# Four heads' 16x16 triangles inverted in one batch, a block per partition, in a two-layer DeltaNet and attention trunk on one core

## The chip, the cores and the metric

The kernel runs on one core of one Trainium2 chip. The number that counts is the device time of one execution in microseconds. A core has TensorE (PE in the profile, with its weight loads as PEld), VectorE (DVE), ScalarE (ACT), GpSimd (POOL) and SyncE (SP); all of them run their own instruction lists in order and wait for each other by semaphores. DMAs are issued from an engine's list, before the change from SP's alone.

## The reference, cut to what matters

Two layers, 256 tokens, width 2048. In each layer the normed and modulated input is projected into the queries, keys, values and gates of eight DeltaNet heads and into sixteen attention heads; both kinds of output are concatenated, projected back and added; then comes a SwiGLU block. The part that the change touches is the inverse of a unit lower triangular matrix for each chunk of each head:

```python
lower = jnp.where(strict, jnp.einsum('bhncd,bhnsd->bhncs', kb, kc) * decay, 0.0) + eye
t_inv = lax.linalg.triangular_solve(lower, jnp.broadcast_to(eye, lower.shape),
                                    left_side=True, lower=True, unit_diagonal=True)
w = jnp.einsum('bhncs,bhnsd->bhncd', t_inv, kb * jnp.exp(gc)[..., None])
u = jnp.einsum('bhncs,bhnsd->bhncd', t_inv, vb)
```

The kernel cuts the 256 tokens into two chunks of 128 and so has two 128x128 triangles per head, each with eight 16x16 triangles on its diagonal.

## The kernel before, in words

All activations lie transposed, 128 features by 256 tokens. A weight block of 128x128 is split into a rounded part `wh` (a CAST on ACT) and the rest `wl` (a subtraction on DVE, sometimes on POOL), 512 columns at a time, and PE multiplies both parts with the split activations: two or three matmuls for a block (`mm2`, L663, and `mm3`, L656). DVE also makes the dot products of the modulation (`wada`, L576), the conv steps, the residual sums and most of the small steps of the heads.

The order of all engines' instructions is fixed when the program is built. `Timed` (L96) keeps a clock for each engine from prices of its own, and `Steps` (L217) holds the heads' steps as generators: at each tick between two weight blocks it lets those run whose engine has room by these clocks, and what they issue then stands at that place in the engine's list. Where the builder has nothing to issue for the next projection, because a buffer or a flag is missing, it calls `S.wait()` (L266), and only steps of the heads are put in until the flag is there. `Weights.split` (L336) puts the casts and subtractions up to five parts of four blocks ahead of PE.

The first layer's early projections are summed in stages while the modulation arrives (L1478). From about 250 us the heads of layer 0 run, then the output projection (`gemm_two`, L1532), then from 653 us the feed-forward block; layer 1 starts at 1377 us, its output projection at about 1768 us, its feed-forward block at 1850 us.

The projections go in the order of `JOBS` (L36 to L38): `ak` and `av` for attention's keys and values, two `aq`, and then for each DeltaNet head `k`, `q`, one `aq`, `v` and `z`. Within a layer the value projection of head h waits until head h-2 has set its flag `mid` (L1525), since the value tile has two buffers.

`delta` (L1163) is one DeltaNet head from its decay factors to its gated output:

- scores: two matmuls `g1`, `g2` with the keys as weights (L1196), then on DVE the norms (`junk`, `sk`), their reciprocal `sc` and the scaled and decayed matrices `B` (L1210). Two heads may be past this point at a time (`head`, `B` with two buffers).
- the triangles: DVE masks the diagonal blocks (`do`, L1228) and sums them into `mc`, 16 columns for each of 128 rows and two chunks (L1232); two more instructions make `R` (L1240), and a matmul with the constant `same` spreads each block's rows over its 16 partitions (L1246).
- the inverse: for each of the 15 columns and two chunks one multiply-and-sum on DVE into `uc` (L1254), and a read of its accumulator; 30 pairs that each need the one two before.
- merging: `U` spreads `uc` into block form (L1264), PE transposes U and the values v (L1275, L1277), and three rounds join blocks of 16 into 32, 64 and 128, with hops from PE to DVE or ACT and back at each (`y16`, `yn`, W).
- the rest: state, output, norm and gate; the matmuls with `V` (L1383) are the first that need the values.

SBUF tiles come from one pool; PSUM has one pool for each stage, `HEADS` and `FFN` (L168).

## Time and profile before

| | |
|---|---|
| median of 3 runs | 2602.87 us (2583.37 to 2609.12) |
| the profiled execution | 2606.06 us |
| its span, first to last instruction | 2604.2 us |
| around the span | 1.9 us |
| mean granted TensorE clock | 0.983 |

A row of a group gives the engine, the operation, output and inputs by the program's names, the shape, the count, the busy time and the mean of one. Since every operation is recorded through one helper, L155 stands at nearly all rows, and tiles tell them apart. A row of a table of stretches gives for each engine its busy time and the number of instructions, then the granted clock and the DMA engines' share. PE's records end by a model, and matmuls overlap in them, so PE's pitch is read from starts.

### The profile page before, as it was taken

What the parts mean: (1) busy time and instruction counts of PE and PEld (TensorE: products, weight loads), DVE (VectorE), ACT (ScalarE), POOL (GpSimd) and SP (SyncE); (2) the same over time, 40 slices, a digit from 0 to 9 for tenths busy, and PEclk for the clock granted to TensorE, in tenths of its full rate; (3) what the DMA queues carried; (4) which work ended last, traced back from release to release, by engine and by line L of the source; (5) the groups of instructions that cost most, each with busy time, mean ns of one, the idle gap of its engine ahead of it and who ended that gap; (6) DMA issues with size and microseconds to landing.
All of it is one profiled execution on the core that took longest, in us unless ns stands there. A gap on an engine that the chain in (4) does not pass through costs nothing.

```text
span 2604.2 us, 45895 instructions
## 1 busy us (share of the span) xinstructions
PE 2500.6 (96%) x16398; PEld 2148.0 (82%) x16398; DVE 1944.2 (75%) x4831; ACT 1281.5 (49%) x2759; POOL 417.9 (16%) x375
## 2 busy tenths in 40 slices
PE   6999999888999999999999899999899999999998
PEld 4777777777888888888888788998788888888887
DVE  3647777998777888888997877787877766555565
ACT  3225555335455444454445565644555544555553
POOL 2223333552000000000003443345000000000000
PEclk9999999999999999999999899999899999999999
DMA  8888664675777899999996433346577766555564
GB/s 279 294 286 290 241 211 171 222 253 187 259 253 252 311 323 323 324 328 330 324 346 204 163 123 121 130 162 203 194 265 249 261 187 188 196 190 188 184 195 137
DMA packets 184088, 608.62 MB, mean 234 GB/s; under 512 B 19121, under 2 KB 30513, under 8 KB 183857
## 3 DMA queue, kind: packets, MB, share of 16 engines
q1 hardware_dynamic: 183858, 605.68, 68.4%
q8 instruction: 128, 2.10, 0.3%
q14 instruction: 102, 0.84, 0.1%
HBM read 603.51 MB, written 2.10 MB: 233 GB/s over the span
## 4 chain that ended last, share of the span: by engine, by line
PE 42%; issue 30%; DVE 6%; ACT 1%; POOL 0%; POOLq 0%; DVEq 0%; ACTq 0%
PE pr L155 19%; PE psm L155 12%; PE pm L155 10%; DVE wl L155 1%; DVE wada L155 1%; DVE x L155 1%; ACT wh L155 0%; DVE act L155 0%; DVE R L155 0%; DVE mc L155 0%; DVE ry L155 0%; DVE sp_y L155 0%; DVE cv L155 0%; DVE do L155 0%; DVE B L155 0%
## 5 line engine op out<-in xcount | busy, mean ns | idle before, releaser
L155 ACT CAST wh<-w 128x512 fp32r<-128x512 f32 (+1 forms) x1566 | 900.9, 605 | 408.1 <-PE psm L155 137.7
L155 DVE TENSOR_TENSOR wl<-w,wh 128x512 fp32r<-128x512 f32 (+1 forms) x1317 | 893.3, 698 | 249.9 <-ACT wh L155 240.0
L155 PE MATMUL pr<-act,wh 128*128 128x512 f32 x2816 | 993.0, 397 | 10.8 <-DVE kq L155 7.5
L155 PE MATMUL pr<-act,wl 128*128 128x256 f32 x2816 | 792.8, 282 | 0.0
L155 PE MATMUL pm<-act,wh 128*128 128x256 f32 (+1 forms) x2816 | 658.6, 320 | 13.8 <-DVE x L155 5.0
L155 PEld LDWEIGHTS pr<-act,wh 128*128 128x128 f32 x2816 | 531.4, 189 | 137.5 <-DVE kq L155 8.1
L155 PE MATMUL psm<-act,wh 128*128 128x512 f32 (+1 forms) x1792 | 569.4, 373 | 1.8 <-ACT wh L155 0.9
L155 POOL TENSOR_TENSOR wl<-w,wh 128x512 fp32r<-128x512 f32 (+1 forms) x249 | 344.3, 1388 | 1272.0 <-ACT wh L155 1174.2
L155 PEld LDWEIGHTS pm<-act,wh 128*128 128x128 f32 x2816 | 462.7, 194 | 88.9 <-issue 44.6
L155 PEld LDWEIGHTS pr<-act,wl 128*128 128x128 f32 x2816 | 535.7, 190 | 0.0
L155 PE MATMUL pm<-act,wl 128*128 128x256 f32 x1664 | 474.3, 285 | 1.3 <-POOL wl L155 1.3
L155 PE MATMUL psm<-act,wl 128*128 128x256 f32 x1600 | 450.5, 282 | 1.7 <-POOL wl L155 1.7
L155 PEld LDWEIGHTS psm<-act,wh 128*128 128x128 f32 x1792 | 325.6, 190 | 72.5 <-issue 9.0
L155 DVE CUSTOM_DVE_ANT_0 wada<-wada,cs 128x1024 f32<-128x1024 f32 x256 | 325.5, 1274 | 36.6 <-DMA wada<-w_ada 36.2
L155 PEld LDWEIGHTS pm<-act,wl 128*128 128x128 f32 x1664 | 322.4, 194 | 2.2 <-POOL wl L155 1.7
L155 PEld LDWEIGHTS psm<-act,wl 128*128 128x128 f32 x1600 | 304.0, 190 | 2.7 <-POOL wl L155 2.1
L155 ACT COPY kq<-pr 128x512 f32<-128x512 f32 x88 | 51.8, 589 | 206.7 <-PE pr L155 206.6
L155 POOL TENSOR_TENSOR n2r<-ms,halfc 128x2 f32<-128x2 f32 x5 | 3.5, 691 | 797.9 <-DVE ms L155 797.9
L155 DVE TENSOR_TENSOR kq<-pr,kq 128x512 f32<-128x512 f32 x88 | 60.6, 688 | 92.8 <-ACT kq L155 92.8
L155 DVE SCALAR_TENSOR_TENSOR x<-psm,mod,x 128x256 f32<-128x256 f32 x128 | 61.9, 483 | 70.4 <-PE psm L155 67.9
L155 PE MATMUL psm<-wada,cs 128*32 128x256 f32 x1024 | 86.7, 414 | 17.7 <-DMA wada<-w_ada 17.5
L155 ACT CAST act<-kq 128x256 fp32r<-128x256 f32 x88 | 35.8, 407 | 74.0 <-DVE kq L155 74.0
(176 smaller groups left out, 1752.1 us busy)
## 6 DMA issues: line engine op xcount, KB each, us to landing
wada<-w_ada SPq DMA_DIRECT2D x384, 512.0 KB, 5.5
w<-w_gu SPq DMA_DIRECT2D x352, 512.0 KB, 4.6
w<-w_in SPq DMA_DIRECT2D x147, 512.0 KB, 4.0
w<-w_dn SPq DMA_DIRECT2D x128, 512.0 KB, 4.6
w<-w_out SPq DMA_DIRECT2D x64, 512.0 KB, 4.3
w<-w_dn SPq DMA_DIRECT2D x64, 384.0 KB, 4.2
w<-w_in SPq DMA_DIRECT2D x28, 384.0 KB, 4.9
x<-xT SPq DMA_DIRECT2D x4, 512.0 KB, 7.5
```

The costliest lines, as they stand in the source:

```text
L155: return f(*a, **k)
```

## The change

`delta` is cut in three. `scores` runs from the decay factors to `mc`, and now also squares the queries and sums them (`sq`, `qn`), so that a head's key and query tile is free after it. `inverses` takes the `mc` of four heads: eight DMAs from ACT's list bring each block of 16x16 into one partition of `qi` (64 partitions, one for each of 4 heads, 2 chunks and 8 blocks); DVE inverts all 64 at once, joining 2x2 into 4x4, 8x8 and 16x16 by products and sums; eight more DMAs from ACT's list bring the result back as `uc`, in the form that it had before. The DMA instructions stand in ACT's list between its casts. The new `delta` starts at `U`, and transposes the values only after the merging, where it also sets `mid`.

`JOBS` puts the keys and queries of four heads first; those of head h+4 come after `v` and `z` of head h. `B` has six buffers in place of two, `y16` two. To have room for it SBUF gets a pool for each stage, like PSUM: the heads' tiles and eight of the feed-forward's `act` tiles (now `mid`) lie in the same place at different times. The constants `same` and `nid16` are gone, and `own` carries the sign. The builder charges 2500 ns for each batch of DMAs (`nc.end += 2500`).

```diff
-NACT = 38
+NACT, NMID = 30, 8
 NEG = -1e30
 
 
-AHEAD = 2
+
+AHEAD, BATCH = 2, 4
 JOBS = [("ak", 0), ("av", 0)] + [("aq", h) for h in range(AHEAD)]
+for _h in range(BATCH):
+    JOBS += [("k", _h), ("q", _h)] + [("aq", AHEAD + _h // 2)] * (_h % 2)
 for _h in range(H):
-    JOBS += [("k", _h), ("q", _h)] + [("aq", _h + AHEAD)] * (_h + AHEAD < H) + [("v", _h), ("z", _h)]
+    JOBS += [("v", _h), ("z", _h)]
+    for _n in range(BATCH, H):
+        if _n - BATCH == _h:
+            JOBS += [("k", _n), ("q", _n), ("aq", _n)]
...
-HEADS = {"pm": 3, "psm": 5}
-FFN = {"pr": 2, "psm": 4}
+HEADS = {"pm": 3, "psm": 5}, {"w3": 5, "B": 6, "z": 3, "dn": 2, "ry": 2}
+FFN = {"pr": 2, "psm": 4}, {"mid": NMID}
+
+HEADS_TOO = {"ak", "vT", "U", "W", "V", "dy", "av", "junk", "yn", "qi", "ui", "uc", "mc", "hi", "y16"}
...
+            yield from b.take("B", N_)
+            yield from b.take("cv", A_)
+            kq = st["kq"]
+            sq = b.t("cv", [128, T])
+            nc.scalar.activation(out=sq, in_=kq[:, 1, :], func=AF.Square)
             yield from b.take("psm", P_, 2)
-            kq = st["kq"]
             g1, g2 = b.bank(), b.bank()
             kqf = kq.rearrange("p a c -> p (a c)")
             nc.tensor.matmul(g1, kq[:, 0, 0:128], kqf, start=True, stop=True)
             nc.tensor.matmul(g2[:, 0:256], kq[:, 0, 128:256], kq[:, :, 128:256], start=True, stop=True)
+            for tb in range(2):
+                nc.tensor.matmul(g2[:, 256 + tb : 257 + tb], sq[:, tb * 128 : tb * 128 + 128], one, start=True, stop=True)
+            b.give("kq")
+            b.give("cv")
...
+            if "mc" not in bt:
+                bt["mc"], bt["n"] = b.t("mc", [128, BATCH, 2, 16], bufs=1), 0
             nc.vector.tensor_reduce(
-                out=mc, in_=mo.rearrange("p a (m c) -> p a c m", c=16), op=ALU.add, axis=mybir.AxisListType.X
+                out=bt["mc"][:, h % BATCH, :, :], in_=mo.rearrange("p a (m c) -> p a c m", c=16), op=ALU.add,
+                axis=mybir.AxisListType.X,
             )
             b.give("do")
+            st.update(B=B, qn=qn, rk=rk)
+            bt["n"] += 1
+            if bt["n"] == BATCH:
+                S.add(inverses(bt, bt["ui"]), 0)
+
+        def inverses(bt, ui):
+
+            yield A_
+            qi = b.t("qi", [64, 272], bufs=1)
+            for x_ in range(2 * BATCH):
+                nc.scalar.dma_start(
+                    out=qi[x_ * 8 : x_ * 8 + 8, 0:256].rearrange("m (i j) -> m i j", j=16),
+                    in_=bt["mc"][:, x_ // 2, x_ % 2, :],
+                )
+            nc.end += 2500
+            yield D_
+            nc.vector.tensor_copy(out=ui[:, 1:256:34], in_=qi[:, 1:256:34])
+            def parts(of, n):
+
+                t = 8 // n
+                v = of.rearrange("p (t r) -> p t r", t=t)[:, :, 0 : 2 * n * 16].rearrange("p t (i c) -> p t i c", c=16)
+                return lambda i, j: v[:, :, i * n : i * n + n, j * n : j * n + n]
+
+
+            yield D_
+            u2, tmp = parts(ui, 2), b.t("hi", [64, 64], bufs=1)
+            v, to = tmp[:, 0:8].rearrange("p (t i) -> p t i", t=4), u2(0, 1)
+            nc.vector.tensor_copy(out=to, in_=parts(qi, 2)(0, 1))
             nc.vector.tensor_tensor(
-                out=mc, in0=mc, in1=C("id16").unsqueeze(1).to_broadcast([128, 2, 16]), op=ALU.subtract
+                out=v, in0=to[:, :, :, 0], in1=u2(1, 1)[:, :, 0:1, 1].to_broadcast([64, 4, 2]), op=ALU.mult
             )
-            R = b.t("R", [128, 32, 16], bufs=1)
+            nc.vector.tensor_tensor(out=to[:, :, :, 1], in0=to[:, :, :, 1], in1=v, op=ALU.add)
+            yield D_
             nc.vector.tensor_tensor(
-                out=R, in0=mc.rearrange("p a c -> p (a c)").unsqueeze(2).to_broadcast([128, 32, 16]),
-                in1=C("nid16").unsqueeze(1).to_broadcast([128, 32, 16]), op=ALU.mult,
+                out=v, in0=to[:, :, 1, :], in1=u2(0, 0)[:, :, 0:1, 1].to_broadcast([64, 4, 2]), op=ALU.mult
             )
-            yield from b.take("psm", P_)
-            q = b.bank()
-            nc.tensor.matmul(q, C("same"), R.rearrange("p c k -> p (c k)"), start=True, stop=True)
-            qk = q.rearrange("p (a c k) -> p a c k", a=2, c=16)
-            yield D_
-            uc = b.t("uc", [128, 2, 16], bufs=2)
-            nc.vector.tensor_copy(out=uc, in_=C("id16").unsqueeze(1).to_broadcast([128, 2, 16]))
-            for c in range(1, 16):
-                for blk in range(2):
-                    junk = b.t("jk", [128, 16], bufs=2)
-                    nc.vector.tensor_tensor_reduce(
-                        out=junk[:, 0 : c + 1], in0=uc[:, blk, 0 : c + 1], in1=qk[:, blk, c, 0 : c + 1], scale=1.0,
-                        scalar=0.0, op0=ALU.mult, op1=ALU.add, accum_out=uc[:, blk, c : c + 1],
-                    )
-                if c % 5 == 0 and c < 15:
+            nc.vector.tensor_tensor(out=to[:, :, 0, :], in0=to[:, :, 0, :], in1=v, op=ALU.add)
+            for n in (4, 8):
+                t = 8 // n
+                tmp = b.t("R", [128, 512], bufs=1)[0:64, 0 : t * n**3].rearrange("p (t i j k) -> p t i j k", t=t, i=n, j=n)
+                half = b.t("hi", [64, 64], bufs=1)[:, 0 : t * n * n].rearrange("p (t i j) -> p t i j", t=t, i=n)
+                qn_, un_ = parts(qi, n), parts(ui, n)
+                for out, lhs, rhs in ((half, qn_(0, 1), un_(1, 1)), (un_(0, 1), un_(0, 0), half)):
                     yield D_
-            b.give("psm")
+                    for x_ in range(t):
+                        nc.vector.tensor_tensor(
+                            out=tmp[:, x_], in0=lhs[:, x_].unsqueeze(2).to_broadcast([64, n, n, n]),
+                            in1=rhs[:, x_].rearrange("p k j -> p j k").unsqueeze(1).to_broadcast([64, n, n, n]), op=ALU.mult,
+                        )
+                        nc.vector.tensor_reduce(out=out[:, x_], in_=tmp[:, x_], op=ALU.add, axis=mybir.AxisListType.X)
+            yield A_
+            uc = b.t("uc", [128, BATCH, 2, 16], bufs=2)
+            for x_ in range(2 * BATCH):
+                nc.scalar.dma_start(
+                    out=uc[:, x_ // 2, x_ % 2, :],
+                    in_=ui[x_ * 8 : x_ * 8 + 8, 0:256].rearrange("m (i j) -> m i j", j=16),
+                )
+            nc.end += 2500
+            bt["uc"] = uc
+
+        def delta(l, h, st, bt, y16, outs):
+
+            while "uc" not in bt:
+                yield N_
+            yield from b.take("head", D_)
+            B, qn, rk = st["B"], st["qn"], st["rk"]
+            MT = B[:, 0, :]
...
+            b.give("psm")
+            while "v" not in st:
+                yield N_
+            yield from b.take("psm", P_)
+            q = b.bank()
+            for tb in range(2):
+                nc.tensor.transpose(q[:, tb * 128 : tb * 128 + 128], st["v"][:, tb * 128 : tb * 128 + 128], ident)
+            st["mid"] = True
+            yield A_
+            V = b.t("V", [128, 2, 128], bufs=2)
+            for tb in range(2):
+                nc.scalar.activation(
+                    out=V[:, tb, :], in_=q[:, tb * 128 : tb * 128 + 128], func=AF.Copy, scale=rk[:, tb : tb + 1]
...
+            y16s = [b.t("y16", [128, 256], bufs=2) for _ in range(2)]
+            for y16 in y16s:
+                nc.gpsimd.memset(y16, 0.0)
+
+            ui = b.t("ui", [64, 272], bufs=1)
+            nc.gpsimd.memset(ui, 0.0)
+            nc.gpsimd.memset(ui[:, 0:256:17], 1.0)
+            sts, bts = {}, [{"ui": ui} for _ in range(H // BATCH)]
+            for kind, h in JOBS:
+                if kind in ("ak", "av"):
+                    project(kind, h, put)
+                    if kind == "av":
+                        S.add(kv_heads(l, kvq, kv), 0)
+                        S.add(betas(l, hs, bgs), 0)
+                elif kind == "aq":
+                    project("aq", h, lambda q, j=h: attention(l, j, q, kv, outs), 0)
+                elif kind == "k":
+                    S.grab(b, "kq")
+                    kq = b.t("kq", [128, 2, T])
+                    st = sts[h] = {"kq": kq, "bg": bgs}
+                    project("k", h, lambda q, h=h, kq=kq, st=st: conv_silu(l, kq[:, 0, :], q, 8 + h, st, "k"))
+                    S.add(scores(l, h, st, bts[h // BATCH]), 0)
+                elif kind == "q":
+                    project("q", h, lambda q, h=h, st=sts[h]: conv_silu(l, st["kq"][:, 1, :], q, h, st, "q"))
+                elif kind == "v":
+                    S.add(delta(l, h, sts[h], bts[h // BATCH], y16s[h % 2], outs), 0)
+                    while h > 1 and "mid" not in sts[h - 2]:
+                        S.wait()
+                    vT = b.t("vT", [128, T], bufs=2)
+                    project("v", h, lambda q, h=h, vT=vT, st=sts[h]: conv_silu(l, vT, q, 16 + h, st, "v"))
+                else:
+                    project("z", h, lambda q, st=sts[h]: gate(q, st))
```

What moves, engine by engine. The whole list loses 16 `same` matmuls on PE, and on DVE 480 column steps with their 480 reads, and 16 each of the makers of `R`, the second `mc` and the first `uc`; it gains on DVE 4 batches of 18 instructions (72), on ACT 64 DMA instructions. The number of all other instructions stays, but for 10 of the subtractions `wl` that go from POOL to DVE and some memsets on POOL.

First place: PE in layer 1, at the transposes of U (`psm<-con,U`). `pm` rows are projections, W, U, y and yn are the merging tiles, B and w the heads' and attention's. Before, at head 6 of the layer:

```order
L155 MATMUL pm_21083<-act_16273,wh_20919 128x256 x2
L155 MATMUL pm_21083<-act_16273,wl_20920 128x256
L155 MATMUL psm_21110<-con_64,U_21058 128x128 x2
L155 MATMUL psm_21110<-con_64,vT_20713 128x128 x2
L155 MATMUL psm_21115<-w_5021_21093,con_64 128x256
L155 MATMUL psm_21115<-w_5021_21093,con_64 128x128 x2
L155 MATMUL pm_21083<-act_16294,wh_20963 128x256 x2
L155 MATMUL pm_21083<-act_16294,wl_20964 128x256
L155 MATMUL pm_21083<-act_16317,wh_20963 128x256 x2
L155 MATMUL pm_21083<-act_16317,wl_20964 128x256
L155 MATMUL psm_21141<-W_21122,B_20831 128x64 x2
```

In the change, at heads 4 and 5 of layer 1, the start and the end of the merging:

```order
L160 MATMUL pm_19951<-act_16099,wh_19916 128x256 x2
L160 MATMUL pm_19951<-act_16099,wl_19917 128x256
L160 MATMUL psm_20050<-con_67,U_20032 128x128 x2
L160 MATMUL psm_20056<-con_67,U_20038 128x128 x2
L160 MATMUL psm_20067<-W_20059,B_17934 128x64 x2
L160 MATMUL psm_20070<-con_67,w_4463_19814 128x128 x3
L160 MATMUL psm_20074<-W_20064,B_18550 128x64 x2
L160 MATMUL psm_20081<-y_3655_16118,U_20032 128x64
```

```order
L160 MATMUL psm_20161<-W_20064,B_18550 64x64 x2
L160 MATMUL psm_20155<-U_20032,yn_20118 64x64 x2
L160 MATMUL psm_20161<-U_20038,yn_20138 64x64 x2
L160 MATMUL psm_20170<-con_67,vT_19662 128x128 x2
L160 MATMUL pm_20175<-act_15772,wh_19936 128x256 x2
L160 MATMUL pm_20175<-act_15772,wl_19937 128x256
```

Before, projections stand between a head's steps (68 to 126 of them between the transposes of U and the first matmul with V). Here two heads go through the merging together, and from the transposes of U to those of the values no projection stands between: the value projection of head 6 waits for `mid` of head 4. At the same place of layer 0, 24 projection matmuls are left in it. Between the last scores of the batch and these transposes stand 198 projection matmuls in layer 1 and 123 in layer 0; for the first batches of the layers it is 162 and 141.

Second place: DVE and ACT in layer 1 at the second batch. In the change ACT has the DMAs between its casts:

```order
L160 COPY cv_19671<-pm_19563 32x256 x4
L160 CAST wh_19691<-w_19531 128x512
L160 DMA qi_19704<-mc_17985 8x16x16 x8
L160 CAST wh_19720<-w_19531 128x512
L160 CAST wh_19739<-w_19576 128x512
L160 CAST wh_19756<-w_19576 128x512
L160 ACTIVATE cv_19765<-pm_19663,par_66 128x256
L160 CAST wh_19777<-w_19613 128x512
```

and DVE, from the sum `mc` of the batch's last head to the first use of `qi`:

```order
L160 TENSOR_REDUCE mc_17985<-do_19698 128x32
L160 TENSOR_TENSOR ry_19672<-pm_19563,con_67 128x256
L160 TENSOR_TENSOR wl_19721<-w_19531,wh_19720 128x512
L160 TENSOR_TENSOR wl_19757<-w_19576,wh_19756 128x512
L160 TENSOR_TENSOR ry_19672<-ry_19672,cv_19671 128x256
L160 TENSOR_TENSOR wl_19778<-w_19613,wh_19777 128x512
L160 SCALAR_TENSOR_TENSOR cv_19765<-pm_19663,par_66,cv_19765 128x255
L160 COPY ui_16122<-qi_19704 64x8
L160 COPY ui_16122<-qi_19704 64x4x2x2
```

and at the end of the inverse, up to U:

```order
L160 TENSOR_TENSOR R_19864<-ui_16122,hi_19865 64x512
L160 TENSOR_REDUCE ui_16122<-R_19864 64x8x8
L160 SCALAR_TENSOR_TENSOR z_19875<-th_19876,pm_19752 128x256
L160 TENSOR_TENSOR wl_19984<-w_19823,wh_19983 128x512
L160 TENSOR_TENSOR wl_20009<-w_19823,wh_20008 128x512
L160 TENSOR_TENSOR U_20032<-uc_19993,con_67 128x128 x2
```

Six instructions stand on DVE between the DMAs' source and their first reader, three of them (`wl_19721`, `wl_19757`, `wl_19778`) behind casts that ACT issues only after its eight DMAs. After the inverse it is three, and the cast for the last of them (`wh_20008`) stands on ACT behind the eight DMAs of `uc`. In the other three batches there are 9, 13 and 11 on the way out and 6, 2 and 2 on the way back.

118 lines of the change are left out of this document (40 added, 78 removed).

## The prediction

> **What bounds the kernel now.** First the page's totals, then the table of stretches cut at the stages.
>
> ```profile
> PE 2500.6 (96%) x16398; PEld 2148.0 (82%) x16398; DVE 1944.2 (75%) x4831; ACT 1281.5 (49%) x2759; POOL 417.9 (16%) x375
> ```
> ```profile
> core 0: us, PE busy (x) PEld busy (x) DVE busy (x) ACT busy (x) POOL busy (x), PEclk, DMA share, GB/s
> 250.00:450.00 200.00, 198.29 (x1748) 153.69 (x1748) 153.12 (x756) 115.82 (x337) 69.76 (x77) 0.98 0.63 212
> 450.00:628.00 178.00, 152.00 (x948) 128.04 (x948) 167.31 (x423) 71.76 (x164) 88.24 (x62) 0.94 0.66 224
> 653.00:1377.00 724.00, 722.43 (x4087) 626.93 (x4088) 608.08 (x1153) 348.83 (x669) 0.97 (x1) 1.00 0.88 307
> 1490.00:1768.00 278.00, 271.36 (x2253) 249.19 (x2252) 213.08 (x904) 155.68 (x416) 104.66 (x104) 1.00 0.40 135
> 1850.00:2604.00 754.00, 737.65 (x4235) 649.51 (x4234) 491.75 (x870) 383.21 (x719) 0.69 (x1) 0.99 0.62 203
> ```
>
> PE bounds nearly everything. In both feed-forward stages it is busy for 98% or more, and the change alters nothing there but which SBUF address eight tiles have. The heads of layer 0 lie in 250 to 628 us, those of layer 1 mostly in 1490 to 1768. In four of these five stretches PE is full and DVE is not; only in 450 to 628 is it the other way: DVE 167 of 178 us, PE 152. So DVE work that goes away pays in that stretch, and elsewhere only where PE waits for it. What PE waits for on this path, first in 250 to 628, then in 1377 to 1768:
>
> ```profile
> PE psm L155 <- DVE U L155: 8.0, 2, 7.2
> PE psm L155 <- DVE R L155: 2.3, 1, 2.3
> ```
> ```profile
> PE psm L155 <- DVE R L155: 3.2, 4, 1.7
> ```
>
> That is 13.5 us for all sixteen heads together, most of it one wait. The builder's order hides the solve almost everywhere behind projections of other heads. The one long wait, and what follows it:
>
> ```profile
> 496.41 0.66 PE L155 MATMUL psm<-con,U 128*128 128x128 f32 x2 [7.18 <-DVE U L155]
> ```
> ```profile
> 488.00:494.00 6.00, 1.23 (x8) 0.81 (x6) 6.00 (x25) 0.00 (x0) 4.31 (x3) 0.96 0.73 268
> 494.00:504.00 10.00, 6.80 (x24) 5.70 (x24) 9.96 (x40) 3.62 (x9) 2.71 (x3) 0.51 0.45 158
> ```
>
> After seven idle microseconds PE gets half its clock for ten. A wait of that length costs PE more than itself; here DVE was full all the while (9.96 of 10), so little of it counts.
>
> **What the change takes away.** On PE the sixteen `same` matmuls. Their records overlap, so I take the pitch from the scores, a pair of the same kind:
>
> ```profile
> 1618.92 1.45 PE L155 MATMUL psm<-kq 128*128 128x512 f32 x4
> 1547.64 11.52 PE pm L155 x96
> ```
>
> A 512-wide and a 256-wide product took 1.45 us; two thirds of it, 0.95 us, is a `same`, and 16 of them 15 us, in a stage where PE is full: on the path. (The second row, of the chain: a projection matmul every 0.12 us.) The waits for R and U, 13.5 us, lose their cause. For the half clock behind the long wait I count 2 of a possible 5 us.
>
> On DVE the solve goes. Its records overlap too; two starts nine steps apart:
>
> ```profile
> 484.37 0.16 DVE L155 CUSTOM_DVE_ANT_0 jk<-uc,psm 128x2 f32<-128x2 f32 x1
> 485.44 0.16 DVE L155 CUSTOM_DVE_ANT_0 jk<-uc,psm 128x6 f32<-128x6 f32 x1
> ```
> ```profile
> L155 DVE TENSOR_TENSOR R<-mc,con 128x512 f32<-128x512 f32 x16 | 12.1, 759 | 0.5
> L155 DVE TENSOR_TENSOR mc<-mc,con 128x32 f32<-128x32 f32 x16 | 7.3, 456 | 0.6
> L155 DVE COPY uc<-con 128x32 f32<-128x32 f32 x16 | 4.2, 263 | 0.0
> L155 DVE TENSOR_REDUCE mc<-do 128x32 f32<-128x256 f32 x16 | 9.6, 601 | 0.6
> L155 DVE TENSOR_TENSOR sp_y<-sp_y,sp_s 128x16 f32<-128x16 f32 x14 | 2.4, 173 | 0.3
> ```
>
> Each step is 0.12 us, 30 are 3.6 us a head; with the other three rows 1.5 us more, so 5.1 us a head and 81 us in all. What is added per batch of four, by the nearest rows: six small ones at 0.17 (`sp_y`), four products of 64 at 0.23 and four sums at 0.25 (between `sp_y` and the 256-wide sum's 0.60), two 512-wide products at 0.76 (`R`) and two sums at 0.85 (twice as wide as `mc`, with its start): 1.0 + 0.9 + 1.0 + 1.5 + 1.7 = 6.1 us, 24 for four. DVE loses 57 us net. In the stretch where it is full that is heads 6 and 7, 10.2 less one batch of 6.1: 4 us gained. Elsewhere I count nothing, for PE is full there; if PE should become the idle one, up to 25 us more.
>
> Together: 15 + 13.5 + 2 + 4 = 34 us gained.
>
> **What it adds.** PE's list is in order, so a late U stops everything behind it: the projections that stand next, the heads', and behind those the feed-forward. Four times, once a batch, PE comes to the transposes of U, and the question is whether U is there. From the last scores of a batch, in head 4 of layer 1:
>
> ```profile
> 1623.53 0.61 DVE L155 TENSOR_REDUCE mc<-do 128x32 f32<-128x256 f32 x1
> ```
>
> `mc` ends 5.2 us after the scores began (1618.92). Then the way out. No DMA of this shape, SBUF to SBUF in pieces of 64 bytes, is in the trace. Nearest rows for the issue (on SP) and the landing:
>
> ```profile
> 79.55 0.33 SPq L115 DMA_DIRECT2D wada<-w_ada  x1
> 1381.55 0.73 SPq L115 DMA_DIRECT2D kq<-w_ba  x1
> ```
> ```profile
> kq<-w_ba SPq DMA_DIRECT2D x2, 256.0 KB, 4.3
> out<-x SPq DMA_DIRECT2D x2, 128.0 KB, 1.8
> mod<-bada SPq DMA_DIRECT2D x1, 96.0 KB, 2.2
> ```
>
> Eight issues of 0.33 us are 2.6, and 2.2 for the last to land: 4.8 us. Bounds: 8 x 0.33 + 1.8 = 4.4, and, if each is like `w_ba` with its 2048 pieces, 8 x 0.73 + 4.3 = 10.1. I take 4.8, since each DMA has 128 pieces, nearer the rows of the small transfers.
>
> The DMA page of the Trainium skill (DMA: Bandwidth & Descriptors, section Bandwidth) speaks against the change: transfers under 64 KB are bound by their descriptors, about 0.68 us each at 4 KB. An estimate by that page, eight one after the other, gives 5.4 + 2.2 = 7.6 us for a way; eight ways at 2.8 us more would make the sum below 22 us worse. No run here shows it.
>
> While ACT issues, its casts wait: in layer 1's second batch three of the six DVE rows that should fill the way out subtract from casts behind the DMAs, so DVE reaches `qi` some 2.5 us after it landed (2.6 us for the DMAs, then three casts of 0.6 and one row of ACT). Then the batch: 18 own instructions, 6.1 us, with 14, 8, 11 and 17 others among them, at DVE's mean of 0.40 us (1944.2 over 4831) 5.6, 3.2, 4.4 and 6.8: 11.1 us in the mean. The way back 4.8, two halves of U 0.6. In all 5.2 + 4.8 + 2.5 + 11.1 + 4.8 + 0.6 = 29 us.
>
> PE's cover from scores to transposes: in layer 1's second batch 198 projection matmuls, 23.8 us, the scores 1.45 and attention's scores about 1.3: 26.5. The others have 162, 141 and 123 (19.4, 16.9, 14.8 us) and 6 to 10 us of other matmuls each, so 23 to 27; mean 25.5. PE waits 29 - 25.5 = 3.5 us, four times: 14. Bounds: nothing behind the casts and ways of 4.4 us gives 1 us, 4 in all; ways of 10.1 us give 14 us, 56 in all.
>
> Then the merging of heads 4 and 5, where the values of head 6 wait for `mid`. Head 12 of the trace, from its U to the last products before V:
>
> ```profile
> 1643.56 0.38 PE L155 MATMUL psm<-con,U 128*128 128x128 f32 x2
> 1657.34 0.44 PE L155 MATMUL psm<-U,yn 64*64 64x64 f32 x4
> ```
>
> 14.2 us, which 72 projection matmuls (8.6 us) filled. Now layer 1 has none there, layer 0 has 24; but two heads' own matmuls and attention's fill some 8 us. I count 4 us lost in layer 1 and 2 in layer 0; between 0, if the hops run fast with nothing else on DVE, and 12.
>
> ACT's 64 issues are 21 us on an engine that is half idle; what a burst of 2.6 us delays are casts that stand up to five parts (7 us of PE) ahead: 2 us, 0 to 6. Half clock behind waits of PE: 3 us, 0 to 8. The ten `wl` from POOL: 7 us of DVE where it has room, 0. The new SBUF pools: a tile waits for the last reader of an earlier stage's, which PE has passed before the stage begins: 0.
>
> Together 14 + 6 + 2 + 3 = 25 us lost.
>
> **The sum.** 2606.06 - 34 + 25 = 2597. This execution stands 3.2 us above the median of the runs, so 2594 against 2602.87: no change that shows. 1% is 26 us, about what a measurement here tells from none (the runs before spread over 25.8 us).
>
> **The rivals.** *DVE's relief reaches PE.* PE's weight loads in 250 to 628 us also stand idle for short times without a named releaser:
>
> ```profile
> PEld psm L155 <- issue: 24.7, 45, 7.5
> PEld pm L155 <- issue: 23.9, 51, 2.1
> ```
>
> That is 48.6 us in 96 pieces, some of which may be lateness of DVE. 57 us of DVE go; if half of that, 28 us, shortens the stages instead of 4, and the ways take 4.4 us (loss 15 in place of 25), the time is 2594 - 24 - 10 = 2560. For it: DVE full in 450 to 628. Against: in 1490 to 1768 PE has 271 of 278 us. It decides when PE's waits at U are under 1 us.
>
> That the ACT queue's DMAs do not queue behind SP's loads is what the same page says (section Queues, rings and completion order: the engines take turns between queues, a packet at a time); that would favour this rival, and the trace, with one queue, cannot show it.
>
> *The ways are long, on the other side.* The small DMAs run beside the weight loads (DMA share 0.4 to 0.66 in the heads' stretches), and at the price of `w_ba` a way takes 10.1 us. Then PE waits 14 us at each U, 56 in place of 14, and with half clocks behind each (8 in place of 3) the time is 2594 + 42 + 5 = 2641. For it: the pieces are the smallest in the kernel, and DVE stands in order behind `qi` and `uc`. Against: 8 KB each. Slower by 1% from a way of about 7.5 us on.
>
> *It does not do what it says to the time.* The solve was hidden already, and the waits for R and U reappear at other tiles, since the builder always leaves some: then only the 15 us of matmuls count against the 25 us lost: 2613.
>
> **How the numbers follow.** Forecast 0.44, relief 0.22, long ways 0.24, hidden anyway 0.10. The forecast and the last are within 1%: 0.54; faster 0.22, slower 0.24. The forecast's own range is 2575 to 2620 (loss 4 + 0 + 0 + 0 to about 40); the whole one reaches to both other cases, 2564 to 2638.
>
> **What would show it.** Right: no `same` and `jk` rows, DVE's busy time down by some 57 us (by its records, which overlap, more), PE's wait for U a few microseconds in each of four places, a PE gap with only merging matmuls in layer 1 shortly before the value projection of head 6, and stretches of feed-forward as before. The DMA table shows the ways: a landing near 2 us and issues of 0.3 us, or otherwise. Wrong: waits at U of 10 us or more, with half clocks behind (the long ways); or 250 to 628 shorter by over 30 us (the relief); or feed-forward stages that change.

## The result and the profile after

The change took 2618.89 us in the median (2608.46 to 2630.49, 20 runs), the kernel before 2601.80 on the same chip (2583.37 to 2616.16, 20 runs). The ratio is 1.0076, 95% interval 1.0055 to 1.0097. The prediction had 2594 us against 2602.87, a gain of 0.3%; it is a loss of 0.8%, some 17 to 20 us. The time lies in the predicted range (2564 to 2638) and the loss is under the 1% that was called no change, but the sign is wrong by more than the measurement leaves open, so something in the sum is wrong and has to be found.

The profiled execution of the change took 2614.97 us, span 2613.2, against a span of 2604.2 before. Its totals:

```profile
PE 2488.9 (95%) x16366; PEld 2145.7 (82%) x16366; DVE 1896.8 (73%) x3905; ACT 1283.7 (49%) x2759; POOL 414.5 (16%) x372
```

PE has 32 instructions fewer and DVE 47 us less; both were to be. PE is busy 12 us less and yet the span is 9 us longer, so PE stands idle 21 us more. To see where, I cut both spans at the same four events: in each layer the first product of its scores and the first product of its feed-forward block (`pr`). The two rows are the heads and output projection of layer 0 and of layer 1, first before:

```profile
244.10:624.30 380.20, 352.49 (x2734) 283.00 (x2732) 321.92 (x1184) 186.99 (x502) 160.11 (x142) 0.97 0.65 220
1462.80:1851.70 388.90, 375.46 (x2929) 339.91 (x2927) 296.94 (x1136) 209.51 (x537) 156.87 (x144) 0.99 0.44 149
```

and after:

```profile
238.30:618.60 380.30, 348.01 (x2722) 285.74 (x2720) 294.49 (x728) 189.31 (x505) 151.43 (x128) 0.96 0.64 221
1452.50:1857.60 405.10, 376.94 (x2911) 345.42 (x2911) 278.65 (x662) 211.53 (x538) 165.45 (x146) 0.96 0.43 144
```

Layer 0's heads take as long as before, layer 1's 16.2 us longer. PE's idle time in the two is 27.7 + 13.4 = 41.1 us before and 32.3 + 28.2 = 60.5 after. Of the other stages, the one up to the first scores is 5.8 us shorter (244.1 to 238.3), and the rest hardly move: the two feed-forward blocks together 1513.4 us before and 1511.7 after, the way from layer 0's end to layer 1's scores 77.6 and 77.9. From here on the sum of the two rows, 769.1 us before and 785.4 after, is called the heads' time. It leaves out the stages that the change doesn't touch, but it comes from one profile of each kernel, so its own spread isn't known; the whole time spreads by 10 to 35 us from run to run.

What PE waits for in the change:

```profile
PE psm L160 <- DMA wada<-w_ada: 21.6, 6, 14.6
PE psm L160 <- DVE U L160: 14.7, 10, 7.7
PE psm L160 <- POOL w L160: 10.2, 3, 9.0
...
PE psm L160 <- ACT W L160: 6.6, 4, 3.8
```

U costs 14.7 us; the prediction had 14. So that term is right in size, and the loss is made of others. (Experiment 2 shows that the size was in part luck. The 14.6 us in the first row, the longest wait for `wada`, lie at the start of the kernel; before the change it was 14.3.) The DMAs themselves, by their issue, minimum, median and maximum in ns, on ACT's queue; the second row is of `uc`:

```profile
L160 ACTq DMA_DIRECT2D qi<-mc x32: 616/620/1242, 281.5 to 1676.5; - x32
```
```profile
L160 ACTq DMA_DIRECT2D uc<-ui x32: 612/612/694, 310.7 to 1700.5; - x32
...
who waited for it (us, times):
  ACT wh L160: 19.2, 3
  PE psm L160: 14.7, 10
```

One issue takes 0.62 us, not 0.33, the 64 together some 40 us. What stands behind a burst in ACT's list begins only after its last issue; what stands ahead may still run beside the first ones. Six of the eight ways hold ACT for 5.3 us. The two ways out of layer 0 take 8.2 and 7.9 us, with gaps between their last issues for which the profile names no cause. By its packets in the trace a way starts to move 1.3 to 1.4 us after its first issue began (once 2.2), and its last packet moves 0.8 to 1.7 us after its last issue ended, so the landing is short and the issue is the way. The packets of all 64 took 0.2% of the DMA engines' time, so they hardly crowd the weight loads. What the hold does is to be seen in layer 1's second batch, on ACT, DVE and PE:

```profile
1696.52 4.56 ACTq L160 DMA_DIRECT2D uc<-ui  x7
1701.12 1.14 ACT L160 CAST wh<-w 128x512 fp32r<-128x512 f32 x2 [4.41 <-DMA uc<-ui]
```
```profile
1695.07 0.68 DVE L160 TENSOR_REDUCE ui<-R 64x64 f32<-64x512 f32 x1
1695.68 0.40 DVE L160 SCALAR_TENSOR_TENSOR z<-th,pm 128x256 f32<-128x256 f32 x1
1696.74 0.69 DVE L160 TENSOR_TENSOR wl<-w,wh 128x512 fp32r<-128x512 f32 x1 [0.66 <-ACT wh L160]
1701.77 0.69 DVE L160 TENSOR_TENSOR wl<-w,wh 128x512 fp32r<-128x512 f32 x1 [4.33 <-ACT wh L160]
1702.38 1.77 DVE L160 TENSOR_TENSOR U<-uc,con 128x128 f32<-128x128 f32 x3
```
```profile
1695.87 0.28 PE L160 MATMUL pm<-act,wl 128*128 128x256 f32 x1
1703.89 1.09 PE L160 MATMUL psm<-con,U 128*128 128x128 f32 x4 [7.74 <-DVE U L160]
```

The inverse is done at 1695.75. The packets of the first DMA are through by 1698, but on DVE a subtraction stands ahead of U whose cast stands on ACT behind all eight issues; U starts at 1702.38, and PE, whose projections ran out at 1696.15, gets 7.74 us of nothing. In layer 0 the same hold reaches PE on another path:

```profile
289.65 1.14 ACT L160 CAST wh<-w 128x512 fp32r<-128x512 f32 x2 [7.45 <-DMA qi<-mc]
```
```profile
282.41 1.00 SPq L120 DMA_DIRECT2D wada<-w_ada  x2
292.24 0.33 SPq L120 DMA_DIRECT2D w<-w_in  x1
```
```profile
SPq L120 <- DVE wl L160: 10.2, 2, 8.8
```
```profile
298.58 1.08 PE L160 MATMUL psm<-wada,cs 128*32 128x256 f32 x8 [4.35 <-DMA wada<-w_ada]
```

ACT's casts stop for 7.45 us (this is one of the two longer ways out), so do the subtractions behind them, so no weight buffer comes free, and SP, whose loads are one list, issues nothing from 283.4 to 292.24 (the third row: SP's waits from 283 to 300 us, 8.8 us of them for one `wl`). Behind the weight load stand the loads of the modulation, and PE waits 4.35 us for one of those. The prediction's term for ACT's bursts, 2 us, doesn't have this path.

### The profile page after: what moved, and what is told of

It is laid out like the page before. It is cut to its first block, busy times and chain, and to the rows that moved or that the text cites. A ratio compares the mean times of both kernels' runs of the same rounds, so it can differ in the third digit from the quotient of the medians.

```text
span 2613.2 us, 44974 instructions
## 1 busy us (share of the span) xinstructions
PE 2488.9 (95%) x16366; PEld 2145.7 (82%) x16366; DVE 1896.8 (73%) x3905; ACT 1283.7 (49%) x2759; POOL 414.5 (16%) x372
## 5 line engine op out<-in xcount | busy, mean ns | idle before, releaser
L160 PE MATMUL pm<-act,wh 128*128 128x256 f32 (+1 forms) x2816 | 647.6, 317 | 13.3 <-ACT act L160 4.5
L160 POOL TENSOR_TENSOR wl<-w,wh 128x512 fp32r<-128x512 f32 x239 | 334.7, 1408 | 1301.4 <-ACT wh L160 1217.8
L160 PE MATMUL psm<-act,wh 128*128 128x512 f32 (+1 forms) x1280 | 391.9, 364 | 1.0 <-DVE mod L160 1.0
L160 PE MATMUL psm<-act,wl 128*128 128x256 f32 x1088 | 305.5, 281 | 1.0 <-POOL wl L160 1.0
L160 PEld LDWEIGHTS psm<-act,wh 128*128 128x128 f32 x1280 | 228.4, 190 | 50.2 <-issue 8.9
L160 PEld LDWEIGHTS psm<-act,wl 128*128 128x128 f32 x1088 | 206.2, 190 | 1.9 <-POOL wl L160 1.5
L160 PE MATMUL psm<-mid,wh 128*128 128x512 f32 x512 | 183.0, 395 | 0.0
L160 PE MATMUL psm<-mid,wl 128*128 128x256 f32 x512 | 144.2, 282 | 0.0
L160 PEld LDWEIGHTS psm<-mid,wh 128*128 128x128 f32 x512 | 96.2, 188 | 22.8
```

The source lines that it names most:

```text
L160: return f(*a, **k)
```

## The experiments

Two theories were set against each other. P: the price is that of the ways, DMAs whose issue holds a queue for 0.62 us each, with what stands behind them. O: the price is that of the order, in which two heads go through the merging with no projection beside them, whatever the ways cost. Experiments are numbered as they ran, in five groups: 1 to 4, 5 to 8, 9 to 11, 12 to 15, and 16. Ratios are to the kernel before, timed beside each group, with their 95% intervals; its medians were 2598.89, 2595.83, 2598.27, 2597.97 and 2601.49 us beside the five. The ratio isn't the ratio of the two medians, and the two differ by up to 0.25%. Experiments 1, 5 and 14 leave out the inverse: what reaches U there is not it.

| | median, us | ratio | heads, layer 0 + layer 1 = sum, us |
|---|---|---|---|
| before | 2601.80 | 1 | 380.2 + 388.9 = 769.1 |
| change | 2618.89 | 1.0076 (1.0055 to 1.0097) | 380.3 + 405.1 = 785.4 |
| 1 copies for DMAs | 2586.96 | 0.9940 (0.9912 to 0.9969) | 360.9 + 392.8 = 753.7 |
| 2 DMAs on SP | 2605.15 | 0.9999 (0.9972 to 1.0026) | 377.6 + 396.2 = 773.8 |
| 3 four value tiles | 2616.41 | 1.0060 (1.0028 to 1.0093) | 372.2 + 398.3 = 770.5 |
| 4 old solve, new order | 2598.71 | 0.9996 (0.9968 to 1.0025) | 371.8 + 393.5 = 765.3 |
| 5 as 1, 16 matmuls more | 2598.02 | 1.0012 (0.9995 to 1.0029) | 366.6 + 395.5 = 762.1 |
| 6 landing in the plan | 2626.20 | 1.0119 (1.0094 to 1.0145) | 384.4 + 407.5 = 791.9 |
| 7 pairs out | 2600.72 | 1.0022 (0.9998 to 1.0045) | 379.0 + 390.1 = 769.1 |
| 8 as 2, landing in the plan | 2610.13 | 1.0059 (1.0037 to 1.0081) | 381.6 + 395.8 = 777.4 |
| 9 half on SP, half on ACT | 2597.86 | 1.0013 (0.9991 to 1.0034) | 367.5 + 400.5 = 768.0 |
| 10 seven `wh`, `wl` | 2635.92 | 1.0155 (1.0124 to 1.0187) | 380.6 + 406.4 = 787.0 |
| 11 pairs out and back | 2613.21 | 1.0053 (1.0026 to 1.0079) | 381.8 + 397.7 = 779.5 |
| 12 two queries later | 2605.07 | 1.0036 (1.0014 to 1.0058) | 375.3 + 397.0 = 772.3 |
| 13 as 12, DMAs as in 9 | 2590.98 | 0.9975 (0.9947 to 1.0004) | 370.1 + 389.3 = 759.4 |
| 14 as 12, copies as in 1 | 2575.97 | 0.9926 (0.9899 to 0.9954) | 359.7 + 382.9 = 742.6 |
| 15 as 12, old solve as in 4 | 2600.88 | 1.0009 (0.9982 to 1.0036) | 375.5 + 391.3 = 766.8 |
| 16 as 13, out in pairs | 2590.19 | 0.9968 (0.9940 to 0.9995) | 361.0 + 390.6 = 751.6 |

**1. Copies for the DMAs.** The plan is charged as for the DMAs, so that every other instruction keeps its place. (The cut is short, with `...` for what is left out of a line.)

```diff
-            for x_ in range(2 * BATCH):
-                nc.scalar.dma_start(out=qi[...], in_=bt["mc"][...])
+            for x_ in range(2):
+                nc.nc.vector.tensor_copy(out=qi[:, x_ * 128 : x_ * 128 + 128], in_=bt["mc"][0:64]...)
...
-                nc.scalar.dma_start(out=uc[...], in_=ui[...])
+                nc.nc.vector.tensor_copy(out=uc[x_ * 64 : x_ * 64 + 64]..., in_=ui[:, x_ * 128 : x_ * 128 + 128])
```

> Leaves out the real inverse: each way's eight DMAs are replaced by two small copies on VectorE, so the values in U are not the inverse; the order of every engine's other instructions is that of the change, row for row. Theory P (price of the ways: ACT issues one of these DMAs in 0.62 us, not 0.33, so a way takes some 5 us of issue, 2 to 3 of landing, and what stands behind it): four batches lose two ways of about 8 us each, so nearly all of PE's waits at U (15 us in the change) and the half clocks behind them go, 25 to 30 us below the change, 8 to 13 us below the kernel before. Theory O (the order: two heads merge with no projection between them, whatever the ways cost): the waits at U go, but PE's idle stretch before the values of head 6 stays; 10 to 15 us below the change, still level with or above the kernel before.

Measured: 0.9940, 32 us below the change in the median (31.7 in the heads' time, 35 by the ratios) and 12 below the kernel before. PE's waits and the two rows of heads:

```profile
PE psm L160 <- DMA wada<-w_ada: 16.8, 6, 14.2
PE psm L160 <- POOL w L160: 9.6, 2, 9.2
...
PE psm L160 <- DVE U L160: 4.9, 6, 2.4
```
```profile
238.20:599.10 360.90, 340.15 (x2721) 279.42 (x2719) 296.09 (x736) 189.90 (x505) 150.65 (x128) 0.98 0.67 232
1429.00:1821.80 392.80, 375.16 (x2912) 344.69 (x2912) 278.95 (x670) 211.41 (x538) 167.22 (x146) 0.96 0.44 148
```

U costs 4.9 us in place of 14.7, so 10 of the 32 us are U. PE's idle time in the heads falls from 60.5 to 38.4 us, and in layer 0 its busy time by 8 us at a higher clock (0.98 against 0.96). P holds; O as the only cause falls.

**2. The same DMAs from SP's queue**, in the same order: `nc.nc.sync.dma_start` for `nc.scalar.dma_start` in both loops.

> The same order, with the 64 issues moved from ACT's queue to SP's. Theory P, if the price is ACT's: SP issues in 0.33 us as it does the loads, ways shorten by 2.5 us each and no cast stands behind them: 15 to 20 us below the change, level with the kernel before. If the price belongs to the DMA's shape, SP needs 0.62 us too, only the casts are freed: 5 to 8 us below the change. Theory O: within 5 us of the change. A third way: the DMAs wait on SP for mc and ui and hold the weight loads back; then slower than the change.

```profile
L1268 SPq DMA_DIRECT2D qi<-mc x32: 597/609/1383, 285.0 to 1673.9; - x32
```

SP needs 0.61 us for one as well: the price goes with the DMA, not with ACT, and SP's 0.33 for a load was the wrong row. Yet the time is that of the kernel before, 14 us below the change in the median (11.6 in the heads' time, 20 by the ratios), where 5 to 8 were expected of this branch. In layer 1 the issues take as long as in the change, 21.2 us for the four ways, and it gains 8.9 of the 11.6 us; so most of the gain comes from ACT being free. (Layer 0's two ways out are 2.7 and 1.8 us shorter.) U's waits are 7.9 us in place of 14.7, and 4.9 of that difference is at the wait shown above, 7.74 to 2.80, where a subtraction with a held cast stood ahead of U on DVE. So nearly half of U's price wasn't the length of the ways. SP is held in ACT's place (one row: eight issues in 5.46 us), and the loads behind them come late: waits for `wada` are up from 16.8 us without DMAs to 23.6.

```profile
PE psm L160 <- DMA wada<-w_ada: 23.6, 9, 14.0
...
PE psm L160 <- DVE U L160: 7.9, 8, 2.8
```
```profile
285.04 5.46 SPq L1268 DMA_DIRECT2D qi<-mc  x8
290.60 0.87 SPq L120 DMA_DIRECT2D wada<-w_ada  x2
```

**3 and 10. Four value tiles, and the room that they took.**

```diff
-                    while h > 1 and "mid" not in sts[h - 2]:
+                    while h > 3 and "mid" not in sts[h - 4]:
...
-                    vT = b.t("vT", [128, T], bufs=2)
+                    vT = b.t("vT", [128, T], bufs=4)
...
-            wh = b.t("wh", [128, 4, 128], F32R, bufs=8)
-            wl = b.t("wl", [128, 4, 128], F32R, bufs=8)
+            wh = b.t("wh", [128, 4, 128], F32R, bufs=7)
+            wl = b.t("wl", [128, 4, 128], F32R, bufs=7)
```

The tenth has only the last four lines of it.

> Four buffers for the value tiles in place of two, so that the values of a head wait for the head four before it and not two: the projections of heads 6 and 7 can stand between the merging of 4 and 5 (room from wh and wl, 7 buffers in place of 8, which alone leaves every order as it was). Theory O: the stretch of PE without projections in layer 1 (about 14 us, half clock) fills; 10 to 15 us below the change. Theory P: the waits at U stay as they are and only the merging's term goes, 3 to 6 us below the change.

> The change with seven buffers for wh and wl in place of eight, the room that the third experiment took for its value tiles; every order is that of the change. That experiment's head stages were 15 us shorter and its feed-forward stages 15 us longer than the change's. If the missing buffer slows the feed-forward: 10 to 15 us above the change (1.012 to 1.013 of the kernel before), and the third experiment's own gain is then some 15 us. If it costs nothing: 1.006 to 1.009, as the change.

By itself the third looked like P (4 us in the ratio). The tenth shows that this was two effects: one `wh` and one `wl` less cost 0.8% with no instruction moved, in the feed-forward and between the layers, and against that base the value tiles gain 0.95%, 16.5 us of the heads' time. So O has a share of its own, beside P.

**4. The old solve in the new order**: `scores` ends with `R`, `same` and the thirty steps, each head has its own `uc`, and `inverses` is gone.

> The new order of projections, the transposes of V late and the pools, with the solve of the kernel before, head by head: the same matmul, R and thirty steps on VectorE, no DMAs. Theory P: the sixteen matmuls (15 us) and 81 us of VectorE come back, the ways go: level with the kernel before, within 6 us of it, since the order costs little. Theory O: the order and its merging cost 10 us or more whatever the solve is: 10 to 20 us above the kernel before, as the change or slower.

0.9996: with the old solve the new order, the late transposes of V and the pools cost nothing (765.3 us of heads against 769.1). But this order is planned around another solve: in layer 1, 123 projection matmuls stand between head 4's U and its values, where the change has none. So it says that the order need not cost, not that the change's order did not. Against experiment 1 it also gives a rough worth of the batch if moving were free, 0.56% or 11.6 us of the heads' time; rough, since the two orders differ.

**5. Sixteen matmuls more**, on top of the copies: the line `nc.tensor.matmul(g1, kq[:, 0, 0:128], kqf, ...)` stands twice.

> The kernel of the first experiment (copies in place of the DMAs, so that the inverse is left out) with the first product of each head's scores issued twice: sixteen more matmuls of 512 columns in fp32, as many and as wide as the ones that the change took away, on PE alone, and the same order everywhere else. If such a matmul costs its pitch, as the prediction had it: 15 us above the first experiment, a ratio to the kernel before of 1.000. If PE has slack there that takes them in: under 5 us, 0.996 or less.

0.72% (19 us) between the two ratios, 11 us between the two medians, 8.4 in the heads' time: the 15 us of the prediction lie within what these allow.

**6 and 8. The landing in the plan**, once with the DMAs on ACT and once on SP:

```diff
             nc.end += 2500
+            yield N_
             bt["uc"] = uc
```

> The change with one line: in the builder's plan the way back now takes its 2.5 us before a head may build its U (the plan of the change drops them, since the generator ends there). The DMAs stay on ACT's queue. Theory P: between 27 and 36 more projection matmuls, some 4 us, stand ahead of U in three of the four batches, and nothing in the fourth; ACT's casts wait as before: 4 to 8 us below the change. If U's wait on its landing were all of the price: 15 us or more below the change.

> The DMAs on SP's queue as in the second experiment, with the landing in the plan as in the sixth. Theory P: both gains add, 20 to 28 us below the change, 0.3 to 0.5% under the kernel before; what is left against the kernel of copies is SP's loads behind qi and the landings. If the two are the same gain: as the second experiment, 0.998 to 1.002.

Both went the other way: 0.4% slower than the change, 0.6% slower than the second experiment. PE's waits for U in the sixth:

```profile
PE psm L160 <- DVE U L160: 21.1, 4, 9.0
```

Four waits of 5 us, in place of ten of 1.5: in the sixth, U comes later against PE than in the change, though the plan knows more of the landing. Why, in these two orders, was not taken apart; it stays open.

**7 and 11. Pairs.** In the seventh the two DMAs of a head leave `scores` as soon as its `mc` stands, the way back leaves in four pairs, and the plan knows issue and landing. In the eleventh each head's way back is a pair of its own at the head of `delta`. Of the seventh, the way out:

```diff
+            yield A_
...
+            for x_ in (h % BATCH * 2, h % BATCH * 2 + 1):
+                nc.clock["scalar"] = max(nc.clock["scalar"], nc.floor) + 320
+                nc.scalar.dma_start(out=bt["qi"][...], in_=bt["mc"][...])
+            nc.end += 2500
+            yield N_
             bt["n"] += 1
```

> Still 64 DMAs on ACT's queue, in pairs: a head's two leave as soon as its own mc stands, the two of the way back leave head by head with other work of ACT between them, and the plan knows their 0.62 us of issue and the landing. Theory P with the burst as its cause (casts, and behind them wl, weight buffers and loads, held for 5 us at a time): the way out shrinks to two issues and a landing, no cast waits over 1.5 us; 15 to 20 us below the change, level with the kernel before or up to 0.3% under it. If what counts is ACT's time in all (42 us of issue), spreading it gives nothing: within 5 us of the change.

> As the seventh experiment, and the way back too in pairs, each issued by ACT when its head is begun (the two batches on the two halves of the partitions, so that no matrix is written over before it has left). No stretch of ACT is held for more than a few pairs. Theory P: layer 1 as in the seventh (390 us from the first scores to the feed-forward) or less, layer 0 comes down from 379 towards the 361 of the copies: 0.995 to 0.999 of the kernel before. If layer 0's loss is not the burst's: 1.001 to 1.003.

The seventh is 14 us under the change by the ratios, 18 by the medians, nearly all of it in layer 1 (405.1 to 390.1 us) and 1 us in layer 0. That is close to what was expected if the bursts are the cause, and far from what was expected if ACT's time in all is. (The eight issues of its way back still run 5.4 to 5.6 us, but ACT begins casts and other work between the pairs.) The eleventh, which parts the pairs further, is slower than the seventh, against both expectations, and layer 0 is no better. Both have orders of their own, so they don't tell bursts from order.

**9. Half on SP, half on ACT**, in the order of the change: `(nc.nc.scalar if x_ % 2 else nc.nc.sync).dma_start`.

> The order of the change, with every second one of the 64 DMAs on SP's queue and the others on ACT's. Theory P: each queue is held 2.6 us a way in place of 5.3, and a way ends 2.6 us sooner; all of U's lateness and most of what stands behind ACT and SP goes: 20 to 28 us below the change, 0.997 to 1.000 of the kernel before. If the two queues do not issue side by side, as the second experiment: 1.000.

1.0013: 21 us below the change by medians, at the poor end of what was expected, and 16 by the ratios, short of it. The eight issues of a way back took 3.0 us in three of the four batches, in place of 5.3; in the fourth, and on the ways out, they still took 5.0 to 5.4. Layer 0 gains 12.8 us, layer 1 4.6; U still costs 11.3 us.

**12 to 15. Filling the merging.** These ask whether O's share is a loss of its own or the late U seen twice. The order of jobs alone is altered; no buffer is added:

```diff
     JOBS += [("v", _h), ("z", _h)]
-    for _n in range(BATCH, H):
-        if _n - BATCH == _h:
-            JOBS += [("k", _n), ("q", _n), ("aq", _n)]
+    if _h < BATCH:
+        JOBS += [("k", _h + BATCH), ("q", _h + BATCH)] + [("aq", _h + BATCH)] * (_h < 2)
+    elif _h < 6:
+        JOBS += [("aq", _h + 2)]
```

> The change with two jobs moved: the attention queries of heads 6 and 7 are projected after the gates of delta heads 4 and 5, not before the values of 2 and 3. In layer 1, 69 projection matmuls then stand before the value transposes of head 4, where the change has none; buffers and DMAs as in the change. Theory P alone (only the ways cost): within 4 us of the change, 1.006 to 1.009 of the kernel before. Theory O beside it (the merging with no projections costs by itself, as the third against the tenth experiment has it, 16 us in the heads' stages): 8 to 16 us below the change, 1.001 to 1.004, nearly all of it in layer 1.

> The same with the DMAs half on SP's queue and half on ACT's, as in the ninth experiment (1.0013). If the two losses are separate they add: 8 to 16 us below the ninth, 0.995 to 0.998 of the kernel before. If they are one loss, seen twice (a late U is what makes the merging stand alone): within 4 us of the ninth, 1.000 to 1.003.

> The same with the copies of the first experiment in place of the DMAs (the inverse is left out). The first experiment, 0.994, with the merging filled: 0.989 to 0.992 if the losses are separate, 0.993 to 0.995 if the merging costs only where U is late.

> The fourth experiment (the solve of the kernel before in the new order, 0.9996) with the two jobs moved. The order there already has projections in every merging stretch, so nothing is expected of the move: 0.997 to 1.002. If it is 0.996 or less, the late attention queries are good for something else than the merging.

| | change's order | two queries later | gain |
|---|---|---|---|
| DMAs on ACT | 785.4 | 772.3 | 13.1 |
| DMAs on both queues | 768.0 | 759.4 | 8.6 |
| copies | 753.7 | 742.6 | 11.1 |
| old solve | 765.3 | 766.8 | -1.5 |

These are heads' times. The gain is there at the full price of the ways, at a part of it, and at none; with the old solve, whose merging had projections already, the two late queries are good for nothing. But not all of the gain is the merging's: U's waits fall too, from 14.7 to 6.7 us with the DMAs on ACT, from 11.3 to 7.5 on both queues and from 4.9 to 1.1 with the copies. That leaves 5, 5 and 7 us for the rest. By medians the first three gains are 14, 7 and 11 us, by the ratios 10, 10 and 4, and 0.9926 for the copies lies between its two expectations. So the whole times alone don't settle it. The stretch itself does, for layer 1: from the transposes of U of heads 4 and 5 to those of the values, in the change, in experiment 1 and in experiment 14:

```profile
1703.89:1717.70 13.81, 12.41 (x110) 10.94 (x110) 8.49 (x31) 4.41 (x13) 0.79 (x1) 0.50 0.21 73
```
```profile
1667.52:1681.34 13.82, 12.42 (x111) 10.95 (x111) 8.49 (x31) 4.41 (x13) 0.80 (x1) 0.50 0.21 73
```
```profile
1656.52:1672.04 15.52, 15.52 (x169) 14.21 (x167) 10.22 (x36) 9.94 (x31) 3.10 (x2) 1.00 0.31 104
```

The merging with no projection takes 13.8 us at a granted clock of 0.50, whatever the ways cost. In experiment 14 it takes 15.5 us at the full clock, and 69 projection matmuls are done in it, 8.3 us at their pitch of 0.12. The empty stretch therefore costs some 6.6 us, a loss of its own that adds to that of the ways. Much of the slow part counts as busy: a PE that is busy for 12.4 of 13.8 us is here at half its clock.

**16. The best of it**: 13 with the way out in pairs as in 7, the plan's price of an issue left as in the change.

> The thirteenth experiment with its way out in pairs: a head's two DMAs leave on ACT's queue as soon as its own mc stands, so that at the end of a batch two issues and a landing are left, and the way back stays half on SP's queue and half on ACT's. If layer 0's rest against the copies (370 against 360 us) and layer 1's (389 against 383) are the bursts of the way out: 0.992 to 0.995 of the kernel before. If pairs only move the hold on ACT and shift the order, as in the eleventh: 0.997 to 1.001.

0.9968 (0.9940 to 0.9995): 0.3% below the kernel before, with the end of the interval just under 1, and 1.1% below the change (medians 2590.19 and 2618.89 us). It lies just outside the second expectation's range and well short of the first, and it isn't clear of experiment 13 (0.9975). Its heads and its wait for U:

```profile
241.40:602.40 361.00, 342.45 (x2721) 280.86 (x2719) 304.07 (x734) 189.86 (x505) 142.26 (x122) 0.97 0.68 233
1431.40:1822.00 390.60, 370.08 (x2912) 339.26 (x2912) 271.82 (x663) 211.83 (x538) 159.99 (x145) 0.98 0.46 150
```
```profile
PE psm L161 <- DVE U L161: 14.6, 5, 7.4
```

Layer 0 is down at 361.0, what the copies had (360.9; 359.7 in experiment 14), and 9.1 us below experiment 13. That fits bursts of the way out as the rest, but it isn't shown: the pairs change the order too, and PE's idle time in layer 0 is 18.5 us in both; what fell is its busy time (351.6 to 342.5 us, at a granted clock of 0.95 and 0.97). Layer 1 is not down (390.6 against 382.9), and U still costs 14.6 us, with one wait of 7.4 in layer 1.

## Why the prediction was wrong, step by step

Two steps failed, and the errors add. The first is the price of an issue: "Eight issues of 0.33 us are 2.6 ... I take 4.8, since each DMA has 128 pieces, nearer the rows of the small transfers", and with it "what a burst of 2.6 us delays are casts that stand up to five parts (7 us of PE) ahead: 2 us, 0 to 6". An issue took 0.62 us, on ACT and on SP. The text had a better bound in hand, 0.73 us for `w_ba`, and put it aside because the bytes were few and the pieces 128. Neither sets the price by itself: a weight load of 128 rows of 4 KB, as most of `w_gu`'s are, also has 128 pieces and issues in 0.33 us. What does set it was not tried. The burst was then 5.3 us and more, twice as long as priced, on the engine whose casts feed the subtractions, the weight buffers and through them SP's list.

The second is "the waits for R and U, 13.5 us, lose their cause", counted in full as time of PE, with 4 us more for DVE. The waits did go, but other waits took much of their place.

The sum redone, from the kernel before to experiment 14 (free ways, merging filled), from there to experiment 1 (free ways) and from there to the change, by medians against the kernel before beside each, by the ratios, and by the heads' times:

| | predicted | medians | ratios | heads' time |
|---|---|---|---|---|
| gains: matmuls, waits for R and U, clock, DVE | -34 | -22 | -19 | -26.5 |
| merging of heads 4 and 5 | +6 | +10 | +4 | +11.1 |
| the DMAs: U, ACT's bursts, clock | +19 | +29 | +35 | +31.7 |
| sum | -9 | +17 | +20 | +16.3 |

(By medians 2575.97 - 2597.97 = -22.0; 2586.96 - 2598.89 = -11.9, so the merging is 10.1; 17.1 - (-11.9) = 29.0.) The three measures differ by up to 8 us in a row, and no row is better known than that. In all three the DMAs cost 10 to 16 us more than priced and the gains are 8 to 15 us smaller: two errors of about the same size.

- *The sixteen matmuls, 15 us*: right within the error (8 to 19 by experiment 5).
- *Waits for R and U, 13.5 us, "lose their cause"*: wrong by about half. Over the whole kernel they were 13.8 us before, and in experiment 14 1.1 are left. Yet PE's idle time in the heads fell only from 41.1 us to 32.8 there, by 8.3 where this term and DVE's had 17.5. Waits for `ry` rose from 3.5 to 8.9 us and those for POOL's `w` from 5.6 to 9.3: the builder left other waits, as the rival "hidden anyway" said. The two rows of experiment 14:

```profile
237.80:597.50 359.70, 341.81 (x2721) 281.09 (x2720) 300.76 (x741) 189.15 (x505) 135.78 (x123) 0.98 0.68 233
1430.50:1813.40 382.90, 368.02 (x2911) 337.98 (x2911) 276.11 (x675) 211.52 (x538) 158.96 (x141) 0.99 0.45 152
```

- *DVE*: 47 us less by its records, predicted 57. The batch's own instructions took longer than the nearest rows had it: 8.5 us a batch and not 6.1, most of it in the products. The two wide ones took 1.82 and 1.09 us in the mean against 0.76; the first took 1.02 us in one batch and 1.99 to 2.14 in the three in which POOL had just begun a subtraction:

```profile
L160 DVE TENSOR_TENSOR R<-qi,ui 64x512 f32<-64x512 f32 x4 | 7.3, 1823 | 0.1
...
L160 DVE TENSOR_TENSOR R<-ui,hi 64x512 f32<-64x512 f32 x4 | 4.4, 1092 | 0.0
```
```profile
306.92 1.02 DVE L160 TENSOR_TENSOR R<-qi,ui 64x512 f32<-64x512 f32 x1
```
```profile
1690.24 2.14 DVE L160 TENSOR_TENSOR R<-qi,ui 64x512 f32<-64x512 f32 x1
```
```profile
1690.09 1.38 POOL L160 TENSOR_TENSOR wl<-w,wh 128x512 fp32r<-128x512 f32 x1 [1.08 <-ACT wh L160]
```

- *PE waits at U, 14 us*: 14.7 by the table of waits, in part by luck. One by one they were not even: layer 1's second batch alone took 7.74 where the mean was put at 3.5, with a chain of 34.7 us (1669.2 to 1703.89) in place of 29 and a cover of 27 as counted. And 6.8 us of the 14.7 went in experiment 2, with ways about as long. For the way out the prediction had counted DVE's wait for held casts, 2.5 us; for the way back, where the list of instructions shows one such cast too, nothing.
- *ACT's bursts, 2 us (0 to 6)*: the mis-sized term. Of the 31.7 us of the heads' time between the change and the copies, PE's idle time is 22.1; 9.8 of that is U, and 12.3 are waits elsewhere, where this term had 2. Moving the same DMAs off ACT's queue at the same order, with ways about as long, gave 11.6 us of the heads' time (6.8 of them at U), though SP's loads paid for it; splitting them over both queues gave 17.4.
- *Half clocks, 3 us (0 to 8)*: the other 9.6 of the 31.7 us are busy time of PE, 8 of them in layer 0 at a granted clock of 0.96 in place of 0.98.
- *Merging, 6 us (0 to 12)*: about right. The table has 4 to 11 us, of which 3.8 are waits for U; the stretch in layer 1 shows 6.6. The place was right; that PE would go through it at half clock the term didn't say.
- *Pools, 0*: nothing against it (the feed-forward blocks 1513.4 and 1511.7 us), and the old solve with the pools and the new order ran at 0.9996.

Three numbers of the prediction don't follow from its own sum, though nothing above hangs on them. "Slower by 1% from a way of about 7.5 us on": eight ways at 4.8 us each stand in the 2594, so 2629 takes ways of about 8.5 us, with the 5 us of half clocks. The upper end of the forecast's own range, 2620 for a loss of about 40, would be 2609. And the whole range, 2564 to 2638, stops short of the two cases that it is said to reach, 2560 and 2641.

The rival of the long ways had the right cause, an issue dearer than 0.33 us, but a price too high and the wrong path: ways of 10.1 us that make PE wait 14 us at each U. The ways were 6 to 7 us, 9 in layer 0's two ways out, and two thirds of what the DMAs cost went round U altogether. The rival "hidden anyway" had 2613 us, the number nearest to 2618.89. It named the right failure of the gains, but its number is near partly by luck: 15 us of gains and 25 of losses, where the runs show 19 to 27 and 39 to 43. The rival of DVE's relief had 2560 us, with 28 us of PE's time from a faster DVE; even with the ways free and the merging filled PE's idle time fell by 8.3.

The Trainium skill (DMA: Bandwidth & Descriptors, section Bandwidth) has 0.68 us for a transfer of 4 KB, from which the prediction estimated a way of 7.6 us and a sum 22 us worse. That row is of loads from HBM issued by GpSimd, and it is the span of the packets. The runs show 0.62 us for the issue alone and the DMAs 10 to 16 us dearer than priced; so the estimate came nearer than the row that I chose, but for another reason. The same page of the Trainium skill, section "Issuing engines are not separate DMA queues", says that starting DMAs from several engines saves only the time of initiating them, usually small beside the DMA itself. Here that time was the price: two queues in place of one took off 16 us by the ratios, 21 by the medians.
